# Second layer's queries projected with channels on the partitions, logits on half-height weights, and a scan's splits cut into pieces

## The chip, the cores and the metric

The kernel runs on one core of a Trainium2 chip. The metric is the device time of one execution in microseconds, and the median of several runs is compared. The core's engines have queues of their own: PE (matmuls, with PEld for loading the stationary operand, the "weights"), DVE and POOL (elementwise work), ACT (elementwise functions and copies) and SP, which issues most DMAs. SBUF is the memory in which tiles lie on 128 partitions; PSUM, eight banks of 512 fp32 columns, is where PE writes.

## The reference

A decoder of two layers on 1024 tokens of 1024 channels: a gated delta-rule layer with 8 heads, then attention over a window of 128 keys with 32 query heads of 64 channels, 4 key heads, a bias by distance and a sink. The queries are normed per head.

```python
# first layer, per head, in chunks: the scan
def step(S, inp):
    qk_i, qd_i, kd_i, u_i, w_i, gl_i = inp
    v_new = u_i - jnp.einsum("bhck,bhkv->bhcv", w_i, S)
    o = jnp.einsum("bhck,bhkv->bhcv", qd_i, S) + jnp.einsum("bhcs,bhsv->bhcv", qk_i, v_new)
    S = S * gl_i[..., None, None] + jnp.einsum("bhck,bhcv->bhkv", kd_i, v_new)
    return S, o
# second layer
q, z = jnp.split(h @ w_in, 2, axis=-1)
q = rms_norm(q.reshape(B, T, B_Q_HEADS, B_HD), q_gain) * (B_HD ** -0.5)
logits = jnp.einsum("bnqkgd,bnskd->bnkgqs", q, k_band) + bias
logits = jnp.where(mask, logits, -jnp.inf)
m = jnp.maximum(jnp.max(logits, axis=-1, keepdims=True), sink)
p = jnp.exp(logits - m)
probs = p / (jnp.sum(p, axis=-1, keepdims=True) + jnp.exp(sink - m))
o = jnp.einsum("bnkgqs,bnskd->bnqkgd", probs, v_band).reshape(B, T, B_W) * jax.nn.silu(z)
return o @ w_out
```

## The kernel before

Large products are made of three matmuls: each operand x is split into a high part hi = x rounded to the matmul's type fp32r and a low part lo = x - hi, and hi hi + hi lo + lo hi is summed in PSUM. Splits take two instructions, a rounding copy (ACT or POOL) and a subtraction (DVE). The normed input lies with channels on the partitions in `hT` (tiles hh and hl, two halves of 512 tokens).

PE's order is written out by hand. `interleave` runs a front generator and a back generator: each `yield` of the front gives a number of units, and the back then emits matmuls worth as many. `later(n, f)` emits f after n more ticks, a tick being one k step of a projection. The other engines' orders are made by a scheduler, from the order of the program, priorities and its own estimate of when operands are ready.

First layer, eight heads (`head_delta`, front; the projections of the next head are the back). After the inverse of each chunk's triangle is merged, `split` (L641) splits the decayed keys `kt` into kth (tile w0) and ktl (tile lt), and the decay-masked q k products `dm` into dmh (w1) and dml, each over all 8 chunks of 128 at once: 128x1024 on POOL (L645), then on DVE (L646). The queries are split likewise, earlier. Then the scan runs over the 8 chunks n: `r`, the new values vh and vl (ACT L804, DVE L805, whose tile is printed as lh), the state's update kth vh + ktl vh + kth vl (L813, L814, L816), and `inside` (L652 to L654), which needs dmh and dml of its chunk one chunk later.

Second layer, eight groups hg of four query heads. `b_order` is the back's order of projections: q of a group (`b_q`) and z, the gate, in two column blocks (`b_z`). `b_q` makes queries with **tokens on the partitions** (`gemm_tc`): the input is the stationary operand, 128x128, and the two query weights move, 256 columns, L971 to L973, 24 matmuls for 128 tokens. They are copied from PSUM (L1095), squared (L1097), summed by head (L1098), and scaled in place by the inverse root (L1103). A weight of a "four" kind has four k steps by 256 columns; `col` has eight by 128.

`b_attend` (front) goes through 64 blocks (X, n), X the group and n the block of 128 tokens. `q_up` splits a block's queries into hi and lo side by side (POOL L1137, DVE L1139), `q_turn` transposes them on PE, four 128x128 transposes (L1146) and a copy (L1149), so that one head's hi and lo lie stacked on 128 partitions. `logits` multiplies them by the high keys (L1167) and the low keys (L1168): eight matmuls, 256 columns (128 when n = 0), into two banks, two heads each. `key_stack` holds each group's keys twice, on partitions 0 to 63 and on 64 to 127. DVE then masks (L1169) and adds the bias, with the minimum over keys against the sink as output m (L1173); logits are kept negated. ACT takes exp with its sum (L1178), POOL multiplies by the inverse sum (L1182), `turn` transposes (L1188), `values` multiplies by v (L1209, 64 columns of the array each, two at a time). The front emits turn(i), q_turn(i+3), q_up(i+4), logits(i+2), values(i-1), with 4.8 units of back in all.

PSUM in the second layer: two banks mm for projections, three tp for transposes, two lg for logits, one pv.

Of the kernel before, what the change touches and what calls it, by code (L numbers as in the profile page):

```python
# [7 lines left out]
F32 = mybir.dt.float32  # L8
# [10 lines left out]
P = 128  # L19
# [45 lines left out]
class Kernel:  # L65
# [122 lines left out]
    def consts(self, ctx):  # L188
# [10 lines left out]
        self.identr = cp.tile([P, P], F32R, name="identr")  # L199
        nc.vector.tensor_copy(self.identr, self.ident)  # L200
# [455 lines left out]
    def head_delta(self, h, H):  # L656
# [23 lines left out]
        qh, ql = self.split(kq[:, :, 1, :], dl, "qh", dl, "ql")  # L680
        nc.gpsimd.tensor_tensor(out=kt, in0=kt, in1=self.kdec[:, :, h:h + 1].broadcast_to([P, NB, P]), op=ALU.mult)
# [87 lines left out]
        kth, ktl = self.split(kt, sm, "w0", dl, "lt")  # L769
        dmh, dml = self.split(dm, sm, "w1", dl, "dml")  # L770
# [18 lines left out]
        for n in range(NB):  # L789
# [21 lines left out]
            if n < NB - 1:  # L811
# [13 lines left out]
                nc.vector.tensor_tensor(out=Sl, in0=S, in1=self.f32(Sh), op=ALU.subtract)  # L825
                yield WAIT["state"]
# [197 lines left out]
    class Group:  # L1024


        def __init__(self, hg):
            self.hg, self.q, self.ot, self.zs, self.left = hg, [], [], [], 5

    def layer_b(self, last):  # L1030
# [7 lines left out]
        for _ in steps:  # L1038
            for _ in range(4):
                next(first)  # L1040
        for _ in first:
            pass
        self.flush()
# [5 lines left out]
        raws = lambda j: bp.tile([P, 2, 512], F32, name="qr", bufs=3)  # L1049
# [11 lines left out]
    def b_order():  # L1061

        z = [("z", hg, j) for hg in range(8) for j in range(2)]
        order = [("q", 0, 0), ("q", 1, 0), z.pop(0)]
# [15 lines left out]
    def b_q(self, X):  # L1080

        nc, bp, sb = self.nc, self.bp, self.sb
        ws = [self.take(), self.take()]
        for half in range(2):
            qr = bp.tile([P, 4, 256], F32, name="qr", bufs=3)
            ss = sb.tile([P, 4, 4], F32, name="ssqb")
            for c in range(4):
                n = half * 4 + c
                if c % 2 == 0:
                    ps = self.mm.tile([P, 2, 256], F32, name="mm")  # L1090
                yield from self.gemm_tc(ps[:, c % 2, :], ws, n)
                if c % 2 == 0:
                    continue
                two = qr[:, c - 1:c + 1, :]
                nc.vector.tensor_copy(two, ps)  # L1095
                sq = sb.tile([P, 8, 64], F32, name="sq", bufs=1)
                nc.scalar.activation(out=sq, in_=two.rearrange("p n (h d) -> p (n h) d", h=4), func=AF.Square)  # L1097
                nc.vector.tensor_reduce(out=ss[:, c - 1:c + 1, :].rearrange("p n h -> p (n h)"), in_=sq, op=ALU.add,  # L1098
                                        axis=AX.X)
            nc.vector.tensor_scalar(out=ss, in0=ss, scalar1=1.0 / 64, scalar2=EPS, op0=ALU.mult, op1=ALU.add)  # L1100
            rq = self.rsqrt(sb, ss, [P, 4, 4], "rqb")
            qv = qr.rearrange("p n (h d) -> p n h d", h=4)
            nc.vector.tensor_tensor(out=qv, in0=qv, in1=rq.unsqueeze(3).broadcast_to([P, 4, 4, 64]), op=ALU.mult)  # L1103
            X.q.append(qv)
# [21 lines left out]
    def b_attend(self, groups):  # L1126
# [3 lines left out]
        qh, qT, Ls, pTs = {}, {}, {}, {}  # L1130

        def q_up(i):
            X, n = blocks[i]
            qv = X.q[n // 4]
            c = n % 4
            t = qh[i] = bp.tile([P, 4, 2, 64], F32R, name="qh")
            nc.gpsimd.tensor_scalar(out=t[:, :, 0, :], in0=qv[:, c, :, :], scalar1=1.0, scalar2=1.0,  # L1137
                                    op0=ALU.mult, op1=ALU.mult)
            nc.vector.tensor_tensor(out=t[:, :, 1, :], in0=qv[:, c, :, :], in1=self.f32(t[:, :, 0, :]),  # L1139
                                    op=ALU.subtract)  # L1140

        def q_turn(i):
            t = qh.pop(i)
            ps = aps.tile([P, 4, P], F32R, name="tp", bufs=3)
            for e in range(4):
                nc.tensor.transpose(out=ps[:, e, :], in_=t[:, e, :, :].rearrange("p a d -> p (a d)"),  # L1146
                                    identity=self.identr)
            qT[i] = bp.tile([P, 4, P], F32R, name="qT")
            nc.scalar.copy(out=qT[i], in_=self.f32(ps))  # L1149

        def logits(i):
# [4 lines left out]
            q = qT.pop(i)  # L1156
            k0 = 0 if n else P
            ksl = slice((n - 1) * P + k0, (n + 1) * P)
            L = Ls[i] = bp.tile([P, 4, P + 1], F32, name="lsb", bufs=3)
            nc.gpsimd.tensor_copy(L[:, :, P:P + 1], sk.unsqueeze(2))  # L1160
# [235 lines left out]
```

## Time and profile before

| | us |
|---|---|
| median of 3 runs | 1869.24 (1867.32 to 1869.59) |
| profiled execution | 1867.8 |
| its span, first to last instruction | 1866.1 |
| PE busy | 1810.6 (97%) |
| PEld busy | 1486.6 (80%) |
| DVE busy | 1219.4 (65%) |
| ACT busy | 834.8 (45%) |
| POOL busy | 527.9 (28%) |

The span has the first layer's heads until about 890 us, its output projection and the shared keys and values until about 1140, the second layer until about 1690, and the last output projection. Busy time of PE is the union of overlapping matmuls: one matmul is listed at 0.28 or 0.39 us while the next starts 0.12 or 0.23 us after it. What a matmul costs is read from start to start. A list of waits names the engine and line that ended each wait of an engine that had nothing else running. The granted clock is a share of 2.4 GHz, and the other level is 1.2.

### The profile page before, as it was taken

The numbers are of one execution on the slowest core, as the hardware profiler recorded it, in microseconds if no ns is written. First come the engines' busy times: TensorE is split into PE (matmuls) and PEld (weight loads), VectorE is DVE, ScalarE is ACT, GpSimd is POOL, SyncE is SP. The second block draws the span as 40 slices with busy tenths as digits, with TensorE's granted clock in tenths as the row PEclk, the third lists the DMA queues.
The fourth block names the chain that finished last, engine by engine and source line by source line (L and its number), as shares of the span: only waits on it lengthen the run. The fifth ranks groups of instructions, "written<-read, shape, count | busy, mean of one in ns | idle before, by whom it ended". The sixth has DMA issues, their size and how long they took to land.

```text
span 1866.1 us, 30785 instructions
## 1 busy us (share of the span) xinstructions
PE 1810.6 (97%) x11650; PEld 1486.6 (80%) x11650; DVE 1219.4 (65%) x2823; ACT 834.8 (45%) x1904; POOL 527.9 (28%) x645
## 2 busy tenths in 40 slices
PE   6999999999999998999999999999999999999999
PEld 6677778787878776778788899888888888877887
DVE  6777776868586778775535365876776776743432
ACT  6446352635445364423112042557667666671100
POOL 0222222323222223221221232434434433321211
PEclk9999999999999999999999999999999999999999
DMA  4611111112011111122655331011112112215552
GB/s 151 132 51 35 57 46 46 47 35 69 24 58 34 58 34 46 46 86 82 240 169 180 114 102 46 30 46 46 57 35 63 55 32 63 68 63 209 181 172 100
DMA packets 134873, 149.54 MB, mean 80 GB/s; under 512 B 7242, under 2 KB 91716, under 8 KB 134724
## 3 DMA queue, kind: packets, MB, share of 16 engines
q1 hardware_dynamic: 124384, 130.40, 22.3%
q10 hardware_dynamic: 10340, 17.16, 3.0%
q8 instruction: 92, 1.51, 0.3%
q14 instruction: 57, 0.47, 0.1%
HBM read 116.05 MB, written 31.49 MB: 79 GB/s over the span
## 4 chain that ended last, share of the span: by engine, by line
PE 76%; DVE 10%; issue 4%; POOL 3%; ACT 1%; DMA 0%; POOLq 0%; ACTq 0%; DVEq 0%
PE mm L182 9%; PE mm L180 9%; PE mm L184 9%; PE acc L920 6%; PE acc L921 6%; PE acc L919 6%; PE mm L971 4%; PE mm L972 4%; PE mm L973 4%; PE pv L1209 3%; DVE acc L494 3%; PE lg L1168 2%; PE lg L1167 2%; PE tp L1188 1%; DVE wlo L157 1%
## 5 line engine op out<-in xcount | busy, mean ns | idle before, releaser
L180 PE MATMUL mm<-hh,whi 128*128 128x512 f32 (+1 forms) x1040 | 427.1, 411 | 2.6 <-ACT hh L246 2.5
L182 PE MATMUL mm<-hl,whi 128*128 128x512 f32 (+1 forms) x1040 | 417.8, 402 | 1.5 <-DVE hl L247 1.5
L184 PE MATMUL mm<-hh,wlo 128*128 128x512 f32 (+1 forms) x1040 | 414.7, 399 | 0.0
L157 DVE TENSOR_TENSOR wlo<-wraw,whi 128x512 fp32r<-128x512 f32 x292 | 209.4, 742 | 221.3 <-POOL whi L150 193.1
L150 POOL TENSOR_SCALAR whi<-wraw 128x1024 fp32r<-128x1024 f32 x110 | 119.8, 1090 | 482.7 <-PE acc L921 242.8
L180 PEld LDWEIGHTS mm<-hh,whi 128*128 128x128 f32 x1040 | 197.3, 190 | 37.7 <-issue 4.6
L184 PEld LDWEIGHTS mm<-hh,wlo 128*128 128x128 f32 x1040 | 197.4, 190 | 35.9 <-issue 4.2
L182 PEld LDWEIGHTS mm<-hl,whi 128*128 128x128 f32 x1040 | 197.6, 190 | 34.2 <-issue 4.2
L971 PE MATMUL mm<-whi,hh 128*128 128x256 f32 x608 | 180.0, 296 | 0.0
L494 DVE SCALAR_TENSOR_TENSOR acc<-u,cw,acc 128x512 f32<-128x512 f32 x192 | 161.7, 844 | 23.5 <-POOL acc L491 21.0
L972 PE MATMUL mm<-wlo,hh 128*128 128x256 f32 x608 | 171.8, 283 | 0.0
L973 PE MATMUL mm<-whi,hl 128*128 128x256 f32 x608 | 171.7, 282 | 0.0
L1178 ACT ACTIVATE lsb<-lsb,m 128x129 f32<-128x129 f32 x256 | 101.0, 397 | 71.3 <-DVE m L1173 42.8
L971 PEld LDWEIGHTS mm<-whi,hh 128*128 128x128 f32 x608 | 115.6, 190 | 10.9 <-issue 10.4
L972 PEld LDWEIGHTS mm<-wlo,hh 128*128 128x128 f32 x608 | 115.8, 190 | 0.2
L973 PEld LDWEIGHTS mm<-whi,hl 128*128 128x128 f32 x608 | 115.6, 190 | 0.0
L153 POOL TENSOR_TENSOR wraw<-wraw,gcolb 128x512 f32<-128x512 f32 x72 | 84.0, 1187 | 111.2 <-DMA wraw<-in_b_w_in 62.6
L1182 POOL TENSOR_TENSOR lsb<-lsb,den 128x512 f32<-128x512 f32 x64 | 69.3, 1082 | 154.1 <-DVE den L1180 134.4
L491 POOL TENSOR_SCALAR acc<-u,cw 128x512 f32<-128x512 f32 x64 | 56.3, 880 | 182.1 <-ACT u L487 168.4
L919 PE MATMUL acc<-whi,hh 128*128 128x512 f32 x256 | 99.7, 389 | 0.0
L921 PE MATMUL acc<-whi,hl 128*128 128x512 f32 x256 | 99.6, 389 | 0.0
L920 PE MATMUL acc<-wlo,hh 128*128 128x512 f32 x256 | 99.6, 389 | 0.0
(352 smaller groups left out, 3872.3 us busy)
## 6 DMA issues: line engine op xcount, KB each, us to landing
wraw<-in_a_w_in SPq DMA_DIRECT2D x48, 512.0 KB, 4.0
wraw<-in_a_w_out SPq DMA_DIRECT2D x32, 512.0 KB, 3.9
wraw<-in_b_w_in SPq DMA_DIRECT2D x32, 512.0 KB, 4.1
wraw<-in_b_w_out SPq DMA_DIRECT2D x32, 512.0 KB, 4.0
og<-zs SPq DMA_DIRECT2D x32, 256.0 KB, 2.0
ogT<-zs SPq DMA_DIRECT2D x24, 256.0 KB, 2.1
btab<-lt SPq DMA_DIRECT2D x1, 4096.0 KB, 24.2
dm<-gd SPq DMA_DIRECT2D x8, 512.0 KB, 3.7
```

The lines of the kernel that those rows point to most:

```text
L150: nc.gpsimd.tensor_scalar(out=hi, in0=raw, scalar1=1.0, scalar2=1.0, op0=ALU.mult, op1=ALU.mult)
L157: nc.vector.tensor_tensor(out=lo[:, ks], in0=raw[:, ks], in1=self.f32(hi[:, ks]), op=ALU.subtract)
L180: nc.tensor.matmul(ps, hi[:, k, :], hh[:, k, :], start=(k == 0), stop=False)
L182: nc.tensor.matmul(ps, hi[:, k, :], hl[:, k, :], start=False, stop=False)
L184: nc.tensor.matmul(ps, lo[:, k, :], hh[:, k, :], start=False, stop=(k == KT - 1))
L494: nc.vector.scalar_tensor_tensor(out=acc, in0=u[:, t:t + 512], scalar=cw[:, t, blk:blk + 1], in1=acc, op0=ALU.mult, op1=ALU.add)
L919: nc.tensor.matmul(ps[c], oh[:, k, ts], hi[:, kk, :], start=(k4 + k == 0), stop=False)
L920: nc.tensor.matmul(ps[c], oh[:, k, ts], lo[:, kk, :], start=False, stop=False)
L921: nc.tensor.matmul(ps[c], ol[:, k, ts], hi[:, kk, :], start=False, stop=(k4 + k == 6))
L971: nc.tensor.matmul(ps, hh[:, k, ts], hi[:, k % 4, :], start=(k == 0), stop=False)
L972: nc.tensor.matmul(ps, hh[:, k, ts], lo[:, k % 4, :], start=False, stop=False)
L973: nc.tensor.matmul(ps, hl[:, k, ts], hi[:, k % 4, :], start=False, stop=(k == KT - 1))
```

## The change

- **Projection.** `b_q` now makes queries with channels on the partitions, as z is made (`gemm_ct`: the weight is stationary, 512 tokens move): per group two weights (pr) by two halves by 24 matmuls of 512 columns. The weights are loaded as `col`. The split comes straight from PSUM: ACT copies to hi (tile qr), DVE subtracts to lo (tile ql). The query transposes, their splits and the rounded identity are gone.
- **Norm.** ACT squares the PSUM tile, DVE transposes it in 32x32 blocks and sums; `b_sums`, some ticks later, adds over partition groups with a small fp32 matmul against a matrix of ones, 64 columns, and makes the inverse root rq and ss = -2 ss' rq (ss' holds half the negated mean square), which is the root. Queries are not scaled any more.
- **Logits.** `rows` multiplies the bias by the root on POOL, into the tile that becomes the logits. `logits` now has twelve matmuls: for each pr, the pairs (qh kh), (ql kh), (qh kl), and in each pair one head on partitions 0 to 63 and one on 64 to 127, so on half-height weights, each head of a pair writing a bank of its own. The DVE step adds the scaled bias to the product, multiplies the sum by rq (scale) and takes the minimum as before.
- **Order.** The front's pieces are turn, logits, rows, values, again with 4.8 units. The first z moves from between q 1 and q 2 to behind q 2, and all others of its kind by one; there is no flush ahead of the attention. Tiles qr and ql have four buffers. The GpSimd DMA scratch is made smaller.
- **First layer.** `split` returns a function for a slice. Queries are split in halves, alternating with the decay of the keys. The keys and dm are split in slices of 2, 2 and 4 chunks: the first key slice ahead of the scan, the others between the scan's first four chunks.

```diff
@@ split
         hi, lo = (p.tile([P, NB, P], F32R, name=t, bufs=1) for p, t in ((ph, hi), (pl, lo)))
-        nc.gpsimd.tensor_scalar(out=hi, in0=x, scalar1=1.0, scalar2=1.0, op0=ALU.mult, op1=ALU.mult)
-        nc.vector.tensor_tensor(out=lo, in0=x, in1=self.f32(hi), op=ALU.subtract)
-        return hi, lo
+        def part(hs):
+            nc.gpsimd.tensor_scalar(out=hi[:, hs], in0=x[:, hs], scalar1=1.0, scalar2=1.0, op0=ALU.mult, op1=ALU.mult)
+            nc.vector.tensor_tensor(out=lo[:, hs], in0=x[:, hs], in1=self.f32(hi[:, hs]), op=ALU.subtract)
+        return hi, lo, part
@@ head_delta
-        kth, ktl = self.split(kt, sm, "w0", dl, "lt")
-        dmh, dml = self.split(dm, sm, "w1", dl, "dml")
+        kth, ktl, part_k = self.split(kt, sm, "w0", dl, "lt")
+        dmh, dml, part_d = self.split(dm, sm, "w1", dl, "dml")
+        part_k(some[0])
...
                 nc.vector.tensor_tensor(out=Sl, in0=S, in1=self.f32(Sh), op=ALU.subtract)
+                if n < 4:
+                    (part_d, part_k, part_d, part_d)[n](some[(0, 1, 1, 2)[n]])
+                if n == 2:
+                    part_k(some[2])
                 yield WAIT["state"]
@@ b_q
+            part = sb.tile([P, 2, 16], F32, name="part")
+            for pr in range(2):
+                ps = self.mm.tile([P, 512], F32, name="mm")
+                yield from self.gemm_ct(ps, ws[pr], half)
+                if pr == 0:
+                    hi = bp.tile([P, 2, 512], F32R, name="qr", bufs=4)
+                    lo = bp.tile([P, 2, 512], F32R, name="ql", bufs=4)
+                nc.scalar.copy(out=hi[:, pr, :], in_=ps)
+                sq = sb.tile([P, 8, 64], F32, name="sq", bufs=1).rearrange("p n d -> p (n d)")
+                nc.scalar.activation(out=sq, in_=ps, func=AF.Square)
+                nc.vector.tensor_tensor(out=lo[:, pr, :], in0=ps, in1=self.f32(hi[:, pr, :]), op=ALU.subtract)
+                sqT = sb.tile([P, 512], F32, name="sqT", bufs=1)
+                nc.vector.transpose(out=sqT, in_=sq)
+                nc.vector.tensor_reduce(out=part[:, pr, :], in_=sqT.rearrange("p (b c) -> p b c", c=32), op=ALU.add,
                                         axis=AX.X)
+            X.q.append((hi, lo))
+            self.later(5, lambda part=part: self.b_sums(X, part))
+
+    def b_sums(self, X, part):
...
+        ps = self.aps.tile([P, 512], F32, name="tp", bufs=3)[:, 0:64]
+        nc.tensor.matmul(ps, self.same, two.rearrange("p r a b -> p (r a b)"), start=True, stop=True)
...
+        rq = self.rsqrt(sb, ss, [P, 4, 4], "rqb")
+        nc.vector.scalar_tensor_tensor(out=ss, in0=ss, scalar=-2.0, in1=rq, op0=ALU.mult, op1=ALU.mult)
+        X.norm.append((rq, ss))
@@ b_attend
+        def rows(i):
             X, n = blocks[i]
...
+            rms = X.norm[n // 4][1][:, :, n % 4:n % 4 + 1]
+            nc.gpsimd.tensor_tensor(out=L[:, :, 0:P], in0=X.bias, in1=rms.broadcast_to([P, 4, P]), op=ALU.mult)
...
+            pss = [aps.tile([P, 2, 256], F32, name="lg") for _ in range(2)]
             for pr in range(2):
-                ps = aps.tile([P, 2, 256], F32, name="lg")
-                for j in range(2):
-                    e = 2 * pr + j
-                    nc.tensor.matmul(ps[:, j, k0:256], q[:, e, :], kh[:, ksl], start=True, stop=False)
-                    nc.tensor.matmul(ps[:, j, k0:256], q[:, e, :], kl[:, ksl], start=False, stop=True)
+                for w, k in ((qh, kh), (ql, kh), (qh, kl)):
+                    for a in range(2):
+                        rs = slice(64 * a, 64 * a + 64)
+                        nc.tensor.matmul(pss[a][:, pr, k0:256], w[rs, pr, :], k[rs, ksl], start=(w is qh and k is kh),
+                                         stop=(k is kl))
...
-        fill = (1.2, 1.2, 0.6, 0.6, 1.2)
+        fill = (2.4, 0.6, 0.6, 1.2)
```

PE's queue before, in the middle of the second layer, at a block's query transposes (mm is a projection's bank, tp a transpose bank, lg a logits bank; numbers are tiles):

```order
L973 MATMUL mm_13259<-whi_12958,hl0_86 128x256
L1146 MATMUL tp_13357<-identr_75,qh_13273 128x128 x4
L971 MATMUL mm_13389<-whi_12770,hh1_87 128x256
L972 MATMUL mm_13389<-wlo_12771,hh1_87 128x256
L973 MATMUL mm_13389<-whi_12770,hl1_88 128x256
```

and, nine projection matmuls later,

```order
L973 MATMUL mm_13389<-whi_12770,hl1_88 128x256
L1167 MATMUL lg_13405<-kh_12625,qT_13271 128x256
L1168 MATMUL lg_13405<-kl_12626,qT_13271 128x256
L1167 MATMUL lg_13405<-kh_12625,qT_13271 128x256
L1168 MATMUL lg_13405<-kl_12626,qT_13271 128x256
L1167 MATMUL lg_13413<-kh_12625,qT_13271 128x256
L1168 MATMUL lg_13413<-kl_12626,qT_13271 128x256
```

PE's queue now, at a block's logits (qr is the high part of the queries, ql the low part):

```order
L182 MATMUL mm_13145<-hl0_83,whi_12766 128x512
L1184 MATMUL lg_13152<-kh_12491,qr_12085 128x256
L1184 MATMUL lg_13153<-kh_12491,qr_12085 128x256
L1184 MATMUL lg_13152<-kh_12491,ql_12086 128x256
L1184 MATMUL lg_13153<-kh_12491,ql_12086 128x256
L1184 MATMUL lg_13152<-kl_12492,qr_12085 128x256
L1184 MATMUL lg_13153<-kl_12492,qr_12085 128x256
```

These six stand there twice, for pr 0 and 1. The transposes have left the queue, the logits fill two banks in turns, and the projections' matmuls are half as many and twice as wide.

DVE's queue before, head 5, from the key split to the state of the scan's first chunk (lt is ktl, w the POOL side of a split, acc the next head's convolution, lh is vl):

```order
L591 TENSOR_TENSOR kt<-kt,rky 128x1024
L646 TENSOR_TENSOR lt<-kt,w_7031 128x1024
L494 SCALAR_TENSOR_TENSOR acc<-u,cw,acc 128x512
L646 TENSOR_TENSOR dml<-dm,w_7035 128x1024
L805 SCALAR_TENSOR_TENSOR lh<-sc,beta,Z 128x256
```

and now:

```order
L589 TENSOR_TENSOR kt<-kt,rky 128x1024
L646 TENSOR_TENSOR lt<-kt,w_7087 128x256 x2
L646 TENSOR_TENSOR lt<-kt,w_7087 128x512
L646 TENSOR_TENSOR dml<-dm,w_7089 128x256 x2
L492 SCALAR_TENSOR_TENSOR acc<-u,cw,acc 128x512
L646 TENSOR_TENSOR dml<-dm,w_7089 128x512
L810 SCALAR_TENSOR_TENSOR lh<-sc,beta,Z 128x256
```

The two subtractions have become six, five of them written behind the first chunk's own work in the program; on the queue all six stand ahead of lh.

## Rows read from the trace of the kernel before

**Rows 1.** Windows: busy us (instructions) by engine, granted clock, DMA share, GB/s.

```profile
60.00:890.00 830.00, 798.83 (x5532) 635.78 (x5531) 605.45 (x1202) 379.89 (x848) 214.34 (x240) 0.99 0.20 55
1140.00:1690.00 550.00, 547.96 (x3797) 463.36 (x3796) 382.46 (x1228) 355.41 (x892) 208.69 (x303) 1.00 0.17 53
1165.00:1170.00 5.00, 4.67 (x29) 4.47 (x28) 5.00 (x17) 1.85 (x9) 3.34 (x4) 0.66 0.00 1
```

**Rows 2.** PE's waits, 1140 to 1690 us: total us, times, longest us.

```profile
PE lg L1167 <- DVE rqbt L118: 0.9, 1, 0.9
PE lg L1167 <- DVE m L1173: 0.8, 1, 0.8
```

**Rows 3.** PE's waits, 60 to 890 us.

```profile
PE sc L816 <- DVE lh L805: 12.1, 15, 1.9
```

**Rows 4.** PE's timeline, a query transpose: start us, duration us, engine, line, operation, tiles.

```profile
1187.35 0.46 PE L1146 MATMUL tp<-identr,qh 128*128 128x128 f32 x4
1187.64 0.35 PE L971 MATMUL mm<-whi,hh 128*128 128x256 f32 x1
1187.83 0.28 PE L972 MATMUL mm<-wlo,hh 128*128 128x256 f32 x1
1187.95 0.28 PE L973 MATMUL mm<-whi,hl 128*128 128x256 f32 x1
```

**Rows 5.** PE's timeline, first logits matmul of a block, first matmul behind the eight.

```profile
1180.90 0.28 PE L1167 MATMUL lg<-kh,qT 128*128 128x256 f32 x1
...
1181.85 0.28 PE L971 MATMUL mm<-whi,hh 128*128 128x256 f32 x1
```

**Rows 6.** PE's timeline, the values matmuls between projection matmuls.

```profile
1190.68 0.28 PE L973 MATMUL mm<-whi,hl 128*128 128x256 f32 x1
1190.88 1.08 PE L1209 MATMUL pv<-pT,vv 128*64 128x256 f32 x8
1191.90 0.39 PE L971 MATMUL mm<-whi,hh 128*128 128x256 f32 x1
1192.12 0.28 PE L972 MATMUL mm<-wlo,hh 128*128 128x256 f32 x1
```

**Rows 7.** PE's timeline, first layer: corner matmuls in pairs, and on one corner.

```profile
236.83 1.15 PE L687 MATMUL kqp<-w 64*64 64x64 f32 x32
...
243.21 1.14 PE L761 MATMUL kqp<-w,lt 64*64 64x64 f32 x16
```

**Rows 8.** PE's timeline, logits of a group's first block, matmul behind them.

```profile
1221.40 0.22 PE L1167 MATMUL lg<-kh,qT 128*128 128x128 f32 x1
...
1222.24 0.33 PE L971 MATMUL mm<-whi,hh 128*128 128x256 f32 x1
```

**Rows 9.** PE's timeline, first layer, around a small ones-matrix matmul.

```profile
150.29 0.39 PE L184 MATMUL mm<-hh,wlo 128*128 128x512 f32 x1
150.52 0.29 PE L552 MATMUL tr<-part,cst 128*128 128x16 f32 x2
150.66 0.47 PE L180 MATMUL mm<-hh,whi 128*128 128x512 f32 x1
150.97 0.39 PE L182 MATMUL mm<-hl,whi 128*128 128x512 f32 x1
```

**Rows 10.** POOL's lines, 1140 to 1690 us: busy us, mean ns, idle before.

```profile
L1182 POOL TENSOR_TENSOR lsb<-lsb,den 128x512 f32<-128x512 f32 x64 | 69.3, 1082 | 154.1 <-DVE den L1180 134.4 <-DVE rqby L111 9.4 <-DVE rqbt L118 9.1
...
L1137 POOL TENSOR_SCALAR qh<-qr 128x256 fp32r<-128x256 f32 x64 | 28.7, 448 | 28.1 <-PE tp L1146 13.7 <-DVE qr L1103 13.1 <-PE tp L1188 1.3
```

**Rows 11.** Timeline of POOL and DVE in head 5, the scan's splits.

```profile
656.24 1.04 POOL L645 TENSOR_SCALAR w<-dm 128x1024 fp32r<-128x1024 f32 x1 [0.96 <-PE kqp L766]
656.28 2.08 DVE L646 TENSOR_TENSOR lt<-kt,w 128x1024 fp32r<-128x1024 f32 x1
...
658.94 1.21 DVE L646 TENSOR_TENSOR dml<-dm,w 128x1024 fp32r<-128x1024 f32 x1
```

**Rows 12.** Lines of the whole span: a DVE split of 256 columns.

```profile
L825 DVE TENSOR_TENSOR XT<-S,X 128x256 fp32r<-128x256 f32 x56 | 24.1, 431 | 15.3 <-ACT X L824 15.3
```

More of the change, by code (lines that the diff above doesn't have):

```diff
@@ L679, in head_delta @@
                                 channel_multiplier=-1)
-        qh, ql = self.split(kq[:, :, 1, :], dl, "qh", dl, "ql")
-        nc.gpsimd.tensor_tensor(out=kt, in0=kt, in1=self.kdec[:, :, h:h + 1].broadcast_to([P, NB, P]), op=ALU.mult)
+        some = (slice(0, 2), slice(2, 4), slice(4, 8))
+        qh, ql, part_q = self.split(kq[:, :, 1, :], dl, "qh", dl, "ql")
+        for hs in (slice(0, 4), slice(4, 8)):
+            part_q(hs)
+            nc.gpsimd.tensor_tensor(out=kt[:, hs], in0=kt[:, hs], in1=self.kdec[:, hs, h:h + 1].broadcast_to([P, 4, P]),
+                                    op=ALU.mult)
         blocks = [(n, r) for n in range(NB) for r in (0, 64)]
@@ L1038, in layer_b @@
         for _ in steps:
-            for _ in range(4):
+            for _ in range(12):
                 next(first)
@@ L1063, in b_order @@
         z = [("z", hg, j) for hg in range(8) for j in range(2)]
-        order = [("q", 0, 0), ("q", 1, 0), z.pop(0)]
+        order = [("q", 0, 0), ("q", 1, 0)]
         for hg in range(2, 8):
@@ L1084, in b_q @@
         for half in range(2):
[L1085 to L1098, printed above, removed]
-                                        axis=AX.X)
@@ new lines, in b_q @@
+            X.q.append((hi, lo))
+            self.later(5, lambda part=part: self.b_sums(X, part))
+    def b_sums(self, X, part):
+        nc, sb = self.nc, self.sb
+        two = sb.tile([P, 2, 2, 16], F32, name="two")
+        first = self.cst[:, C_TRI + 63:C_TRI + 64]
+        nc.vector.tensor_scalar(out=two[:, :, 0, :], in0=part, scalar1=first, scalar2=None, op0=ALU.mult)
+        nc.vector.tensor_tensor(out=two[:, :, 1, :], in0=part, in1=two[:, :, 0, :], op=ALU.subtract)
+        ps = self.aps.tile([P, 512], F32, name="tp", bufs=3)[:, 0:64]
+        nc.tensor.matmul(ps, self.same, two.rearrange("p r a b -> p (r a b)"), start=True, stop=True)
+        two = two.rearrange("p r a b -> p (r a) b")
+        nc.vector.tensor_tensor(out=two, in0=ps.rearrange("p (e b) -> p e b", e=4), op=ALU.mult,
+                                in1=self.group.unsqueeze(1).broadcast_to([P, 4, 16]))
+        ss = sb.tile([P, 4, 4], F32, name="ssqb")
+        nc.vector.tensor_reduce(out=ss, in_=two.rearrange("p e (n g) -> p e n g", g=4), op=ALU.add, axis=AX.X)
+        nc.vector.tensor_scalar(out=ss, in0=ss, scalar1=1.0 / 64, scalar2=EPS, op0=ALU.mult, op1=ALU.add)
+        rq = self.rsqrt(sb, ss, [P, 4, 4], "rqb")
+        nc.vector.scalar_tensor_tensor(out=ss, in0=ss, scalar=-2.0, in1=rq, op0=ALU.mult, op1=ALU.mult)
+        X.norm.append((rq, ss))
@@ L1129, in b_attend @@
         blocks = [(X, n) for X in groups for n in range(NB)]
-        qh, qT, Ls, pTs = {}, {}, {}, {}
-        def q_up(i):
+        Ls, pTs = {}, {}
+        def rows(i):
             X, n = blocks[i]
[L1134 to L1149, printed above, removed]
+            L = Ls[i] = bp.tile([P, 4, P + 1], F32, name="lsb", bufs=3)
+            nc.gpsimd.tensor_copy(L[:, :, P:P + 1], self.sink[:, 4 * X.hg:4 * X.hg + 4].unsqueeze(2))
+            rms = X.norm[n // 4][1][:, :, n % 4:n % 4 + 1]
+            nc.gpsimd.tensor_tensor(out=L[:, :, 0:P], in0=X.bias, in1=rms.broadcast_to([P, 4, P]), op=ALU.mult)
         def logits(i):
@@ L1215, in b_attend @@
         last = len(blocks) - 1
[L1216 to L1218 removed]
+        rows(0)
+        rows(1)
         yield 1.0
         logits(0)
[L1221 to L1222 removed]
+        rows(2)
         yield 1.5
         logits(1)
[L1225 to L1226 removed]
         yield 2.5
[L1228 removed]
+        fill = (2.4, 0.6, 0.6, 1.2)
         steps = iter(())
@@ L1232, in b_attend @@
             yield fill[0]
-            if i + 3 <= last:
-                q_turn(i + 3)
-            if i + 4 <= last:
-                q_up(i + 4)
-            yield fill[1]
             if i + 2 <= last:
                 logits(i + 2)
-            yield fill[2]
+            if i + 3 <= last:
+                rows(i + 3)
+            yield fill[1]
             if X.hg < 7:
@@ L1364, in weights @@
                 for k in range(2):
-                    yield four(bin_, k, hg, gain(2 + k))
+                    yield col(bin_, 2 * hg + k, self.gcolb[:, 8:16])
             else:
```

42 lines of the change are left out of this document (14 added, 28 removed).

## The prediction

> **What bounds the kernel now.** I read the windows first, then PE's waits by stage, then PE's timeline step by step. The windows split the program into the first layer's heads (60 to 890 us) and the second layer (1140 to 1690 us) [rows 1]. In the second layer PE is busy 547.96 of 550 us while DVE, ACT and POOL are busy 382, 355 and 209 us. Only three PE waits are listed there, two of which are shown, 0.9 and 0.8 us, both of logits matmuls as the attention starts [rows 2]. They are followed by a stretch whose granted clock is 0.66 [rows 1], so part of it ran at 1.2 GHz instead of 2.4. Apart from that PE hardly waits: **the second layer is as long as the steps on PE's queue**, and an instruction removed from another engine buys nothing there. In the first layer PE is busy 799 of 830 us; the largest single wait is L816 for the low half of the new values (`vl`, printed as lh, L805), 12.1 us in 15 waits [rows 3].
>
> Busy times of matmuls overlap, so I price PE by the distance from one start to the next.
>
> **Query transposes removed.** Each block's four L1146 transposes take from 1187.35 to 1187.64, 0.29 us. The projection matmul after them also starts its successor 0.19 us later instead of 0.12 [rows 4]. That is 0.36 us a block, 64 blocks: **-23 us**. The copies, splits and casts that go with them are off the path.
>
> **Logits by rows.** Before, eight matmuls of 256 columns take 1180.90 to 1181.85, 0.95 us, or 0.119 us each, with no extra step at either end [rows 5]. Now there are twelve, in six pairs. One of a pair uses rows 0 to 63 of the array, the other rows 64 to 127, each writing a bank of its own. The price hangs on two things that no row shows for this shape.
>
> First, whether the two of a pair run side by side. The nearest rows: L687, 32 fp32 matmuls in pairs on two 64x64 corners of the array, spans 1.15 us, and L761, 16 of them on one corner, spans 1.14 us [rows 7]. The second corner costs nothing, in its loads of weights or in its columns. But those pairs differ in their columns as well as their rows; the new ones share all 128 columns. I take side by side, the side that the rows are nearer to: six pairs, 0.71 us.
>
> Second, what entering and leaving half an array costs. The values matmuls (L1209) use half the columns. The last projection matmul before them lasts 0.20 us instead of 0.12, and after them the first lasts 0.22 instead of 0.12 [rows 6]. An exit step is hidden in their 1.02 us; I give it the price of the entry, 0.09. Together 0.28 us a block. So the new logits cost 0.99 against 0.95, +0.04 for 56 blocks. The eight first blocks of a group have 128 columns and take 1221.40 to 1222.24, 0.84 us or 0.105 each [rows 8]. They become 0.63 + 0.28 = 0.91. Together **+2.8 us**. With no switching cost at all it would be 56 x (0.71 - 0.95) + 8 x (0.63 - 0.84) = -15; with no overlap 56 x (1.43 + 0.28 - 0.95) + 8 x (1.26 + 0.28 - 0.84) = +48. Those are the ends.
>
> On the switching, the Trainium skill, "TensorEngine Tiling (Array Packing)", section Key Properties, says that a change of tiling mode drains TensorE. The steps around L1209 agree; by the rule the logits come out at +2.8, without it at -15.
>
> **Projection turned.** A group's queries were 192 matmuls of 256 columns at 0.119, 22.8 us; now 96 of 512 columns. Row L184 of 512 columns hands over after 0.23 us [rows 9], 22.1 us. Eight groups: -5.6 by rounded steps; I take **-5 us**.
>
> **Norm sums added.** Sixteen small fp32 matmuls (`b_sums`). The nearest row is L552, the same ones matrix with 16 columns: 150.52 to 150.66, and the next step 0.31 instead of 0.23 [rows 9], 0.22 us. With 64 columns between that and 0.30; at 0.24 that is **+3.8 us**.
>
> **Work behind PE in the second layer.** POOL gains one multiplication of 128x512 a block, nearest row L1182 at 1082 ns, and loses L1137 at 448 ns [rows 10]: +41 us on 209 of 550 busy. DVE loses the PSUM copy, the scaling and the query split, and gains a subtract, a transpose, a reduce and the small sums, about as much as it loses. ACT loses 64 copies. All stay below PE, so I cost this at nothing; the cover is the distance of two blocks between a block's logits and its transposes, less than two periods of 550 / 64 = 8.6 us. Both logits banks now go to one block at once, so a block's DVE work on them must end before the next block's first pair, not its second half. All of DVE's work is 382 / 64 = 6.0 us a block, of which this is a part. At the start of the attention the second logits will wait for the first block's DVE work, as before [rows 2]. I put 0 there, with 3 us either way, since a wait of that size decides whether the half-clock stretch comes.
>
> **Pieces in the first layer.** The aim is plain: `vl` is behind the splits on DVE's queue. But the second order excerpt shows all the pieces still ahead of it in a typical head: the scheduler moves what is ready. So nothing is taken off the queue; the pieces only change its cost. At head 5, POOL's split (1.04 us at 656.24) holds up DVE's, which takes 2.08 us beside it and 1.21 alone [rows 11]: the two do not run side by side, so finer pieces are not simply a finer pipeline. A piece of 256 takes 448 ns on POOL [rows 10] and 431 on DVE [rows 12]. Against a quarter of 1.04 and 1.21 that is 0.19 and 0.13 us of fixed cost a piece. Two more pieces in each of two splits: up to 1.27 us a head later, +10 us over eight heads. The other end: DVE waits only for a half after POOL's last piece, 1.21 - (0.61 + 0.13) = 0.48 us earlier a head, -4 us. The middle is +3; I take **+1.5 us**, since the fixed part of a piece on one of the two engines can pass while the other has its turn.
>
> **Sum.** -23 + 2.8 - 5 + 3.8 + 0 + 1.5 = -19.9 us. The profiled execution took 1867.8 us, so 1847.9; the median of the runs is 1869.24, 1.4 us more. Forecast **1849 us**.
>
> **Rivals.**
> - *The pairs run one after the other.* For it: the two share the columns, and the 128-column logits show that 0.105 us is the floor for a matmul with a new 128-column weight, whatever it multiplies [rows 8]. Against it: the corner pairs [rows 7]. Price: +48 instead of +2.8, so 1849 + 45 = **1894 us, slower**. It decides from the point where the second of a pair adds 0.06 us, half its own time: 20 us over 64 blocks of six pairs is 0.05. Beside it, the Trainium skill, "TensorE: Matmul & The Clock Gate", section LDWEIGHTS (loading the stationary operand), says that a load goes by its columns and not its rows, so half-height weights load no faster. The floor of rows 8 fits that; whether two such loads overlap no run here shows.
> - *Switching costs nothing for rows:* -15 instead of +2.8, **1831 us**. Against it the steps around L1209 [rows 6].
> - *The pieces cost their full fixed part:* +10 instead of +1.5, **1857 us**. The waits of L816 [rows 3] would become more than 15.
> - *The second layer waits for POOL or DVE:* if half of the 0.63 us that POOL gains a block lands on PE, +20 us, **1869 us**, no change; all of it, 1889. Against it the shares of rows 1.
> - *The pieces do what they are for:* at most all 12.1 us of the waits for `vl` go [rows 3], instead of +1.5: 1835 us. The order speaks against it; it lies in the range.
>
> **How the numbers follow.** Forecast with its own spread (1835 to 1857) 0.58, of which the last rival has 0.05; no switching cost 0.10; pieces dear 0.12; pairs in turn 0.12; second layer waiting 0.08, half of it slower and half the same. A measurement of this kernel tells about 0.2%, 3.7 us, from no change. Faster by more: 0.58 + 0.10 + 0.12 = 0.80, less 0.01 for both dear at once, 0.79; slower 0.12 + 0.04 = 0.16; same 0.05. The range leaves out the pairs in turn and most of the waiting, 0.18, and below it 0.02: 1830 to 1866 us.
>
> **What would show it.** In the timeline after, a pair's two starts a few ns apart and pairs about 0.12 us from each other mean side by side. Steps of 0.11 to 0.12 for each matmul mean in turn. The steps next to the logits should read about 0.2 and 0.22 where now there are 0.12; no L1146 rows; projection steps of 0.23. In the list of waits, L816 near 12 us, no wait of a logits or transpose matmul beyond the first blocks, and the second layer's PE still busy for 99% of it, at the full clock. I am wrong if the attention's length falls by less than 15 us while the pairs overlap, since then something else than PE has become the bound there, or if the first layer's end moves by more than 10 us.

## The result, and the profile after

The changed kernel takes **1895.82 us** (median of 4, 1893.85 to 1897.71) against 1868.85 (4 runs beside it): ratio **1.0147**, 95% interval 1.0135 to 1.0159. It is slower by 27 us, where 20 us less were forecast. The profiled execution took 1896.8 us, its span 1895.0.

The loss lies in the second layer. From its first key matmul (L971, now L981) to the last values matmul it took 606.1 us before (1081.5 to 1687.6) and takes 636.2 (1080.1 to 1716.3). The scan ends 1.4 us earlier, and the last projection takes 174 us in both.

The windows of the profile after, to set beside [rows 1]:

```profile
core 0: us, PE busy (x) PEld busy (x) DVE busy (x) ACT busy (x) POOL busy (x), PEclk, DMA share, GB/s
60.00:890.00 830.00, 799.29 (x5534) 637.15 (x5534) 606.48 (x1244) 381.06 (x851) 231.15 (x287) 0.99 0.19 56
1140.00:1720.00 580.00, 548.79 (x3092) 393.97 (x3091) 390.35 (x1263) 337.20 (x861) 239.89 (x303) 0.97 0.17 51
```

PE's work in the second layer is 548.8 us, as much as before, but it now stretches over 580 us, and the granted clock is 0.97 where it was 1.00. PE's waits there, against [rows 2]:

```profile
PE tp L1122 <- DVE two L1120: 29.1, 13, 5.6
PE lg L1184 <- DVE m L1192: 2.1, 2, 1.8
```

**L1122 is the matmul of the norm sums.** Thirteen of its sixteen calls make PE stand still for 29.1 us in all, up to 5.6 at a time. PE's queue at one of them:

```profile
1236.40 0.40 PE L182 MATMUL mm<-hl,whi 128*128 128x512 f32 x1
1236.63 0.40 PE L184 MATMUL mm<-hh,wlo 128*128 128x512 f32 x1
1241.16 0.69 PE L1122 MATMUL tp<-two,cst 128*128 128x64 f32 x2 [4.13 <-DVE two L1120]
1241.61 0.77 PE L180 MATMUL mm<-hh,whi 128*128 128x512 f32 x1
```

and DVE's in the same stretch:

```profile
1235.67 0.69 DVE L1215 TENSOR_TENSOR pT<-tp,cst 128x512 f32<-128x512 f32 x1 [0.69 <-PE tp L1207]
1237.35 0.22 DVE L1127 TENSOR_REDUCE ssqb<-two 128x16 f32<-128x64 f32 x1 [0.98 <-POOL lsb L1165]
1237.48 0.68 DVE L1105 TENSOR_TENSOR ql<-mm,qr 128x512 fp32r<-128x512 f32 x1
1238.08 0.16 DVE L1128 TENSOR_SCALAR ssqb<-ssqb 128x16 f32<-128x16 f32 x1
1238.16 0.70 DVE L1108 STREAM_TRANSPOSE sqT<-sq 128x512 f32<-128x512 f32 x1
1238.89 0.69 DVE L1109 TENSOR_REDUCE part<-sqT 128x16 f32<-128x512 f32 x1
1239.61 0.48 DVE L1119 TENSOR_SCALAR two<-part,cst 128x32 f32<-128x32 f32 x1
1240.13 0.98 DVE L1120 TENSOR_TENSOR two<-part,two 128x32 f32<-128x32 f32 x1
```

ACT copied the projection's bank from 1234.47 on. PE has no more than five ticks of other work until L1122 and reaches it at 1236.86. The operand `two` needs the transpose, the reduce and two small steps on DVE, which itself first waits for a transpose of the attention and then for POOL, in L1127, the step that writes the norm tile of the half before: `two` is there at 1241.11. With nothing in the way (the first call, at 1146.0) the chain still takes 3.65 us from ACT's copy; in the attention it takes 4.1 to 8.9.

The wait has a second price. The first projection matmul behind it lasts 0.77 us, where it lasts 0.47 without the wait (e1 below, at 1150.96), and the next one 0.63 instead of 0.39. The window around them:

```profile
1239.80:1246.60 6.80, 5.44 (x21) 4.10 (x22) 2.39 (x6) 0.00 (x0) 1.26 (x2) 0.51 0.01 2
```

The granted clock is 0.51 here, 1.2 GHz. It was 1.00 up to 1239.9, when PE had stood still for about 3 of the 4.1 us. The second layer now has seven such stretches, 34 us in all, where before it had one of 3.4. At half the clock that is 17.0 us lost now and 1.7 before. Five of the seven, 13.6 us lost, begin in or just behind the five longest waits of L1122, 3.4 to 5.6 us each. Of the other two, one comes at the start of the attention, as before, and one at 1089.7, ahead of the attention. PE stands still for 3.6 of the 34 us, so 1.8 of the 17.0 us are in the waits as well.

What was forecast to come did come: no query transposes, projection steps of 0.23 us, and the pairs side by side:

```profile
1404.88 0.40 PE L184 MATMUL mm<-hh,wlo 128*128 128x512 f32 x1
1405.21 0.39 PE L1184 MATMUL lg<-kh,qr 64*128 64x256 f32 x2
1405.43 0.28 PE L1184 MATMUL lg<-kh,ql 64*128 64x256 f32 x2
1405.55 0.28 PE L1184 MATMUL lg<-kl,qr 64*128 64x256 f32 x2
1405.67 0.28 PE L1184 MATMUL lg<-kh,qr 64*128 64x256 f32 x2
1405.79 0.28 PE L1184 MATMUL lg<-kh,ql 64*128 64x256 f32 x2
1405.91 0.28 PE L1184 MATMUL lg<-kl,qr 64*128 64x256 f32 x2
1406.12 0.50 PE L180 MATMUL mm<-hh,whi 128*128 128x512 f32 x1
1406.45 0.39 PE L182 MATMUL mm<-hl,whi 128*128 128x512 f32 x1
1406.69 0.40 PE L184 MATMUL mm<-hh,wlo 128*128 128x512 f32 x1
```

A pair (x2) starts as one, and pairs follow at 0.12 us, as six of [rows 5] would. But the block costs more: from 1404.88 to 1406.69 are 1.81 us, less three projection steps of 0.23 leaves **1.11 us**, where 0.99 was forecast. The price of the half-height form shows in four steps, not three: 0.33 ahead, 0.22 in the first pair, 0.21 behind the last, 0.33 in the next projection matmul, 0.39 us beyond the plain steps.

### The profile page after: what moved, and what is told of

The parts are those of the page before. It is cut to its first block, busy times and chain, and to the rows that moved or that the text cites. A ratio compares the mean times of both kernels' runs of the same rounds, so it can differ in the third digit from the quotient of the medians.

```text
span 1895.0 us, 29395 instructions
## 1 busy us (share of the span) xinstructions
PE 1810.5 (96%) x10914; PEld 1416.1 (75%) x10914; DVE 1227.4 (65%) x2894; ACT 816.0 (43%) x1872; POOL 576.7 (30%) x693
## 5 line engine op out<-in xcount | busy, mean ns | idle before, releaser
L180 PE MATMUL mm<-hh,whi 128*128 128x512 f32 (+1 forms) x1296 | 537.0, 414 | 2.5 <-ACT hh L244 2.5
L182 PE MATMUL mm<-hl,whi 128*128 128x512 f32 (+1 forms) x1296 | 523.9, 404 | 1.5 <-DVE hl L245 1.5
L184 PE MATMUL mm<-hh,wlo 128*128 128x512 f32 (+1 forms) x1296 | 521.6, 402 | 0.0
L180 PEld LDWEIGHTS mm<-hh,whi 128*128 128x128 f32 x1296 | 247.9, 191 | 55.0 <-issue 9.7
L184 PEld LDWEIGHTS mm<-hh,wlo 128*128 128x128 f32 x1296 | 246.9, 191 | 52.5 <-issue 8.1
L182 PEld LDWEIGHTS mm<-hl,whi 128*128 128x128 f32 x1296 | 247.5, 191 | 49.1 <-issue 7.3
L1192 DVE CUSTOM_DVE_ANT_0 lsb<-lg,lsb,sink 128x128 f32<-128x128 f32 x256 | 90.5, 404 | 0.2
L929 PE MATMUL acc<-whi,oh 128*128 128x512 f32 x192 | 76.0, 396 | 0.0
L931 PE MATMUL acc<-whi,ol 128*128 128x512 f32 x192 | 75.9, 395 | 0.0
L930 PE MATMUL acc<-wlo,oh 128*128 128x512 f32 x192 | 75.6, 394 | 0.0
```

The costliest lines, as they stand in the source:

```text
L180: nc.tensor.matmul(ps, hi[:, k, :], hh[:, k, :], start=(k == 0), stop=False)
L182: nc.tensor.matmul(ps, hi[:, k, :], hl[:, k, :], start=False, stop=False)
L184: nc.tensor.matmul(ps, lo[:, k, :], hh[:, k, :], start=False, stop=(k == KT - 1))
L929: nc.tensor.matmul(ps[c], oh[:, k, ts], hi[:, kk, :], start=(k4 + k == 0), stop=False)
L930: nc.tensor.matmul(ps[c], oh[:, k, ts], lo[:, kk, :], start=False, stop=False)
L931: nc.tensor.matmul(ps[c], ol[:, k, ts], hi[:, kk, :], start=False, stop=(k4 + k == 6))
```

## The experiments

"e1" below is the first kernel, which the later ones build on. All ratios are against the kernel before.

**1. The place of the sums (e1), the norm tiles, both.**

```diff
-            self.later(5, lambda part=part: self.b_sums(X, part))
+            self.later(14, lambda part=part: self.b_sums(X, part))
```

> The norm sums are put 14 ticks behind their half's projection instead of 5; nothing else differs from the changed kernel. Theory (sums too early in PE's queue): the small matmul L1122 stands only 5 ticks of 0.69 us, 3.5 us, behind the last projection matmul of its half, while its operand needs ACT's copy and square (0.56 + 0.59) and DVE's transpose, reduce and two small steps (0.70 + 0.69 + 0.24 + 0.19) after it, 3.0 us with no other work in the way; DVE has other work, so PE waited 29.1 us in 13 waits, and half-clock stretches followed. 14 ticks are 9.7 us: the waits of L1122 fall below 3 us, the half-clock stretches in the second layer go with them, and the time is about 1852 us (1846 to 1860). Rival (norm tiles held): DVE's reduce L1127 waits for POOL's rows L1165, 24.7 us in 11, since the norm tile ssqb has two buffers and the rows of two halves back must have read theirs; DVE's queue then holds up the next half's chain. By it a later matmul takes away only a part: PE still waits 10 to 20 us, about 1875 to 1885 us. Third (clock alone, not the waits, or something else in the attention): no change from 1896.

Measured: **1856.65 us** (1854.22 to 1859.30), ratio 0.9938 [0.9923, 0.9953]. One number takes away 39 us. L1122 now stands 9 to 20 us behind the start of ACT's copy, against chains of 3.7 to 10.6, and no wait of it is left in the list:

```profile
PE lg L1184 <- DVE m L1192: 4.7, 3, 3.4
PE tp L1207 <- POOL lsb L1201: 0.8, 1, 0.8
PE lg L1184 <- DVE two L1120: 0.8, 1, 0.8
```

The time lost to the clock in the second layer falls to 3.4 us. And without its wait the small matmul costs what was forecast, 0.24:

```profile
1150.58 0.40 PE L184 MATMUL mm<-hh,wlo 128*128 128x512 f32 x1
1150.82 0.33 PE L1122 MATMUL tp<-two,cst 128*128 128x64 f32 x2
1150.96 0.47 PE L180 MATMUL mm<-hh,whi 128*128 128x512 f32 x1
1151.27 0.39 PE L182 MATMUL mm<-hl,whi 128*128 128x512 f32 x1
```

1150.58 to 1151.27 is 0.69, less two projection steps: 0.23 us.

```diff
-        ss = sb.tile([P, 4, 4], F32, name="ssqb")
+        ss = sb.tile([P, 4, 4], F32, name="ssqb", bufs=4)
-        rq = self.rsqrt(sb, ss, [P, 4, 4], "rqb")
+        rq = self.rsqrt(sb, ss, [P, 4, 4], "rqb", bufs=4)
```

> The two norm tiles (ss and the inverse root) get four buffers instead of two; the sums stay 5 ticks behind the projection. Theory (norm tiles held by POOL's rows): DVE's wait of L1127 on POOL's L1165, 24.7 us in 11, goes to zero, the chain behind it on DVE runs on time, the waits of L1122 fall from 29 us to below 8, and the time is about 1855 us (1850 to 1866). Rival (sums too early in PE's queue): DVE's wait goes all the same, but the chain of 3.0 us still stands behind DVE's other work and meets a slot 3.5 us behind the projection, so PE still waits 15 us or more in L1122: 1875 to 1893 us.

Measured: 1884.69 us (1883.20 to 1886.06), 1.0088 [1.0072, 1.0103]. DVE's wait in L1127 (24.7 us in 11 in the changed kernel) is gone, and PE's wait shrinks, but stays:

```profile
PE tp L1122 <- DVE two L1120: 18.9, 13, 3.1
```

So the norm tiles were a real part, 11 us, but most of the wait is there without them. With both edits:

> Both edits together: 14 ticks and four buffers of the norm tiles. If the waits of L1122 and the half-clock stretches behind them are all that stands between the forecast and the result, this is the forecast, 1849 us (1843 to 1855), whichever of the two edits does it. If the time stays above 1860, a further cost that I have not named is in the second layer.

Measured: 1858.27 us (1858.01 to 1860.85), 0.9949 [0.9935, 0.9964], the same as e1. Once PE comes late enough, it doesn't matter that DVE waits for POOL in L1127 (13.9 us in 6 in e1, none in e3_both). Both stay above the forecast by 8 to 9 us, for which the ledger below accounts.

> Norm sums 9 ticks behind their projection (5 in the changed kernel, 14 in e1_delay14); nothing else. Theory (a slot that comes too early in PE's queue, against a chain on ACT and DVE of a given length): each of the waits of L1122 gets shorter by the 4 ticks, 2.8 us, or vanishes. The gaps ahead of L1122 in the changed kernel, less 0.33 us, were 5.6, 4.5, 4.2, 4.0, 3.5, 3.0 and ten under 1.7 us; what is left is about 8 us in 6, and the half-clock stretches behind the short ones go: 1862 to 1872 us. If the sums' place does not matter above some point, or the waits come from something that follows the matmul wherever it is, as the norm tiles would, the waits stay above 15 us and the time above 1878.

Measured: 1859.43 us (1858.22 to 1860.75), 0.9953 [0.9939, 0.9968]. Better than I expected, with 2.0 us of waits left instead of 8:

```profile
PE tp L1122 <- DVE two L1120: 1.3, 2, 1.0
PE tp L1122 <- DVE rqbt L117: 0.7, 1, 0.7
```

I had counted four ticks as 2.8 us; the attention's own matmuls lie between ticks, so in the trace L1122 now mostly stands 7 to 10 us behind the start of ACT's copy, against chains of 3.7 to 8.8. The dose orders as the theory says: 1896, 1859, 1857 at 5, 9 and 14 ticks, though the last two agree within their spread.

**2. The price of the half-height logits.** All on e1.

```diff
-            for pr in range(2):
-                for w, k in ((qh, kh), (ql, kh), (qh, kl)):
-                    for a in range(2):
+            for a in range(2):
+                for pr in range(2):
+                    for w, k in ((qh, kh), (ql, kh), (qh, kl)):
```

> The kernel of e1_delay14 with the same twelve logits matmuls in another order: the six of the heads on partitions 0 to 63 first, then the six on 64 to 127, so that only one pair of neighbours lies on different rows. It prices the overlap of pairs alone. If pairs side by side are worth a step of 0.117 us each, five of the six are lost: 5 x 0.117 x 56 + 5 x 0.113 x 8 = 37 us over e1_delay14, about 1894 us. If the order of the twelve does not matter, 1857 us.

Measured: 1875.20 us (1872.11 to 1877.88), 1.0042 [1.0028, 1.0056]: 18.5 us over e1, half of what I expected. The timeline tells why:

```profile
1250.71 0.38 PE L1184 MATMUL lg<-kh,qr 64*128 64x256 f32 x1
1250.93 0.28 PE L1184 MATMUL lg<-kh,ql 64*128 64x256 f32 x1
1251.05 0.28 PE L1184 MATMUL lg<-kl,qr 64*128 64x256 f32 x1
1251.06 0.39 PE L1184 MATMUL lg<-kh,qr 64*128 64x256 f32 x2
1251.28 0.29 PE L1184 MATMUL lg<-kh,ql 64*128 64x256 f32 x2
1251.40 0.29 PE L1184 MATMUL lg<-kl,qr 64*128 64x256 f32 x2
1251.51 0.28 PE L1184 MATMUL lg<-kh,qr 64*128 64x256 f32 x1
```

In the queue stand six matmuls of one half, then six of the other. In the trace three run alone, three beside three, three alone: nine steps, not eleven. Three steps more than e1 are 22 us over 64 blocks; PE's waits are 2.5 us shorter than in e1 (3.8 for 6.3), and the clock takes 1.7 us less. The order of issue took away only half of the overlap, so I took away all of it by the operands:

```diff
-                        rs = slice(64 * a, 64 * a + 64)
+                        rs = slice(0, 64)
```

> The kernel of e1_delay14 with all twelve logits matmuls on partitions 0 to 63, in the same order; the second head of each pair gets the first one's logits, so the output is other than the reference's. It takes the overlap away altogether: twelve steps instead of six. In e6_in_turn the trace showed nine steps instead of six (the matmuls on rows 64 to 127 started after three of the other half, though six stood ahead of them), and 18.5 us more than e1_delay14. Six more steps are 6 x 0.117 x 56 + 6 x 0.113 x 8 = 45 us: 1901 us. If a step's length came from something else than the rows, 1857 to 1875.

Measured: **1900.40 us** (1897.61 to 1901.93), 1.0170 [1.0154, 1.0186], 43.8 over e1. On one half of the rows the pairs come 0.24 us apart instead of 0.12:

```profile
1288.67 0.40 PE L1184 MATMUL lg<-kh,ql 64*128 64x256 f32 x2
1288.91 0.40 PE L1184 MATMUL lg<-kl,qr 64*128 64x256 f32 x2
```

Running side by side is worth 44 us here.

```diff
+                nc.tensor.matmul(pss[0][:, pr, k0:256], qh[:, pr, :], kh[:, ksl], start=True, stop=False)
+                nc.tensor.matmul(pss[0][:, pr, k0:256], ql[:, pr, :], kh[:, ksl], start=False, stop=True)
+                nc.tensor.matmul(pss[1][:, pr, k0:256], qh[:, pr, :], kl[:, ksl], start=True, stop=True)
```

> The kernel of e1_delay14 with six logits matmuls over all 128 rows in place of the six pairs: the two heads' products are summed, so the logits are not those of one head and the output is other than the reference's; banks, columns and what reads them stay. It prices entering and leaving the half-height form. The trace of e1_delay14 has 1.11 us a block for six pairs (0.09 before, 0.10 in the first pair, 0.09 behind the last, 0.11 in the next projection matmul over six steps of 0.119): without these the block is 0.71, so 56 x 0.40 + 8 x 0.35 = 25 us less than e1_delay14, about 1831 us. By the prediction's 0.28 a block it is 18 us less, 1839. If entering and leaving costs nothing that the end sees, 1857.

Measured: 1836.19 us (1831.72 to 1839.58), 0.9827 [0.9809, 0.9846], 20.5 below e1, between the two expectations. By its steps the block is 0.40 us shorter (1.40 for logits and three projection steps, 1.81 in the excerpt further up), 25 us in all:

```profile
1257.15 0.40 PE L182 MATMUL mm<-hl,whi 128*128 128x512 f32 x1
1257.38 0.28 PE L1181 MATMUL lg<-kh,qr 128*128 128x256 f32 x1
...
1258.55 0.39 PE L182 MATMUL mm<-hl,whi 128*128 128x512 f32 x1
```

Of that 3.8 us come back as waits of PE (10.1 where e1 has 6.3), and 1.7 by the clock. So 0.39 us a block is the price of the form, and four fifths of it reach the end.

```diff
-        fill = (2.4, 0.6, 0.6, 1.2)
+        fill = (2.4, 0.0, 0.0, 2.4)
```

> The kernel of e1_delay14 with the projection work of a block parted otherwise: units 2.4, 0, 0, 2.4 in place of 2.4, 0.6, 0.6, 1.2, so that the half-height logits of one block and the half-width values of another stand side by side on PE, with no full-size projection matmul between them. In e1_delay14 each of the two pays its own way out and in: behind the logits 0.09 in the last step and 0.11 in the next projection matmul, ahead of the values 0.09, then 0.05 in the first pair. If PE goes from one form to the other in a single step of 0.1 to 0.2 us, 0.15 to 0.25 us a block are saved, 10 to 16 us: 1841 to 1847. If it must empty itself twice, 1857. Against it: DVE and ACT get a block's logits and transposes closer together, and a new wait of PE on them could take all of it: above 1857.

Measured: **1853.00 us** (1850.93 to 1853.90), 0.9916 [0.9901, 0.9931], the lowest median that still computes the reference, 3.6 below e1, though the two intervals overlap. PE does go from one form to the other in one short step:

```profile
1268.96 0.28 PE L1184 MATMUL lg<-kl,qr 64*128 64x256 f32 x2
1269.17 1.08 PE L1228 MATMUL pv<-pT,vv 128*64 128x256 f32 x8
1270.19 0.50 PE L180 MATMUL mm<-hh,whi 128*128 128x512 f32 x1
```

From the last pair 0.21 to the values, and no step of 0.33 between: beyond plain projection steps, logits and values together take 2.11 us instead of 1.11 + 1.21, 0.2 less, 13 us over 64 blocks. Most of it was given back, 1.7 us by the clock (5.1 against 3.4) and 5.3 as waits, 11.6 us where e1 has 6.3:

```profile
PE lg L1184 <- DVE m L1192: 6.1, 6, 3.4
PE tp L1207 <- POOL lsb L1201: 3.9, 6, 1.9
PE lg L1184 <- DVE two L1120: 1.6, 2, 0.8
```

I then moved the transposes, with units 1.6, 0, 0, 3.2:

> As e9_adjacent, with the units of projection work parted 1.6, 0, 0, 3.2: the transposes of a block come 0.8 us later against its logits, which stay beside the values. e9_adjacent saved 0.20 us on PE in each block, 13 us by the steps of its trace, but came out only 3.6 us faster than e1_delay14, with 3.9 us of waits of the transposes for POOL's division (0.8 before) and 7.7 us of waits of the logits (5.5 before). If the waits of the transposes are a matter of distance, those 3.9 us go and the time is 1847 to 1851 us. If the two sorts of waits only change places, 1853.

Measured: 1856.28 us (1852.88 to 1861.64), 0.9939 [0.9924, 0.9953]: no gain. The waits for POOL fell from 3.9 to 0.3 us, those of the logits rose from 7.7 to 11.9. They changed places. That also says what is next behind PE: a block's way through DVE, ACT and POOL no longer fits everywhere in the distance that PE leaves it.

**3. The start of the attention, and the first layer.**

```diff
         rows(2)
-        yield 1.5
+        yield 5.5
         logits(1)
```

> The kernel of e1_delay14 with 5.5 units of projection work in place of 1.5 between the first two blocks' logits. In e1_delay14 the second block's logits wait 3.4 and 1.0 us for DVE's step on the first block, as both logits banks hold that block, and a half-clock stretch of some 7 us follows, 3.4 us of PE's time. If that wait is the cause of the stretch, both go: 8 us less, about 1849 us. If the 4 us of projection work that were moved ahead are missed at the end of the attention, 4 us of it come back: 1853. If the stretch comes anyway, 1853 too, but with the granted clock showing it.

Measured: 1864.28 us (1861.09 to 1868.22), 0.9977 [0.9968, 0.9987], **7.6 slower** than e1. The waits up to 1250 shrank from 5.5 to 3.5 us, but between 1250 and 1550 there are 7.2 us, where e1 has 0.8, and at the end the last two blocks' values stand alone:

```profile
1677.31 1.08 PE L1228 MATMUL pv<-pT,vv 128*64 128x256 f32 x8
1678.86 1.08 PE L1228 MATMUL pv<-pT,vv 128*64 128x256 f32 x8 [0.47 <-ACT ot L1230]
```

Projection work used up early is missing later. The half-clock stretch came all the same, 3.4 us instead of 6.8. All in all PE's waits are 12.2 us against 6.3 and the clock takes 1.7 us less, which is 4.2 of the 7.6; the rest is open.

The pieces of the first layer, put into the kernel before:

> The kernel before with only the first layer's splits cut in pieces, everything else as it was. My step: +1.5 us against the kernel before, from -4 to +10. The first layer of the changed kernel ended 1.4 us earlier than before, with 10.8 us in 14 waits of the last state matmul for vl instead of 12.1 in 15; if that is the pieces' doing, this run is 1 to 2 us faster than the kernel before, about 1867.5 us. The rival that the pieces take vl's waits off: 1857 us, with those waits near zero. The rival that each piece pays its full fixed part: 1878 us.

Measured: 1866.34 us (1862.32 to 1869.66), 0.9989 [0.9979, 0.9999]; and taken out of e1:

> The kernel of e1_delay14 with the first layer's splits whole again, as in the kernel before. e4_pieces alone was 1.7 us faster than the kernel before, interval 0.9979 to 0.9999. If that is the pieces' doing, this run is 1 to 3 us slower than e1_delay14, 1858 to 1860 us. If the pieces cost the 1.5 us of the prediction, it is faster, 1855. The waits of the last state matmul for vl tell how: 12 us in 15 whole, about 11 in 14 in pieces.

Measured: 1859.21 us (1856.22 to 1861.09), 0.9949 [0.9935, 0.9963], 2.6 over e1. Both point to a gain of about 2 us, but neither is far from noise: e4_pieces' interval ends at 0.9999, and that of e11_whole_splits overlaps e1's. The waits for `vl` that the pieces were meant to remove hardly change. They are 12.1 us in 15 with whole splits ([rows 3], and again in e11_whole_splits), and in e4_pieces

```profile
PE sc L823 <- DVE lh L812: 10.9, 14, 2.2
```

## Why the prediction was wrong

- **What bounds the kernel** was right: the second layer is as long as PE's queue. What I did not draw from it is that whatever is put *into* that queue with an operand of another engine becomes part of the bound.
- **Norm sums** is the step that failed. I priced sixteen matmuls, +3.8 us, from a row of the first layer [rows 9], and they cost 0.23 us each, as said. I gave no wait to them. Yet the diff says `later(5, ...)`: five ticks of 0.69 us, while the operand's chain was ACT's copy and square and four DVE steps. The trace before could price it: its first layer has the same transpose and reduce, at 0.70 and 0.68 us (L546, L548), and a square on ACT takes 0.63 (L1097). That comparison, distance against chain, was left out. It cost 29.1 us directly, and moving the sums alone took 39 us off (e1).
- **"I cost this at nothing; the cover is the distance of two blocks"** covered the wrong chain. It held for logits to transposes, which wait nowhere in the list of the changed kernel (its logits wait 2.1 us for m). The sums had a cover of their own, 3.5 us, and I never named it.
- **Half clock.** I allowed 3 us for a stretch at the start. The waits made five more: 17.0 us lost in all instead of 1.7.
- **Logits by rows:** mechanism right, size wrong, +9.9 instead of +2.8 (56 x 0.16 + 8 x 0.12). Side by side was right, and the price I gave for the other case, 45 us, is what e10_one_half measured (43.8). Switching is 0.39 instead of 0.28 us: I took an entry and two exits and left out the first pair's own step. The values had shown it: within the 1.02 us of [rows 6], which I called hidden, the trace has steps of 0.27, 0.22, 0.22 and 0.31. By the Trainium skill, "TensorEngine Tiling (Array Packing)", section Key Properties, a change of mode drains TensorE. The trace agrees in so far as each change costs a step, 0.39 us for the way there and back.
- **Projection** and **query transposes** came as forecast: no rows of the latter, steps of 0.23 for the former.
- **Pieces:** -1.7 and -2.6 instead of +1.5, inside the -4 to +10 given, with the sign on the other side. As forecast nothing was taken off the queue: in the trace after, seven of eight heads run all pieces of the keys and of dm ahead of the scan's first vl.
- **The sign of being wrong** that I had set came: the second layer's length did not fall by 15 us but grew by 30, while the pairs overlap. What took PE's place there was the chain on ACT and DVE.
- **Rivals.** The result lies at the 1894 of *pairs in turn*, but by chance: in the changed kernel no pair ran in turn. What happened is nearest to *the second layer waits for POOL or DVE*, at another place, with some 43 us (waits and clock) where I gave 20 or 40, and with a chance of 0.08.

The ledger closes: -23 (transposes) + 9.9 (logits) - 5 (projection) + 3.7 (sums) + 29.1 (their waits) + 15.3 (clock) - 1.7 (pieces) = +28.3, or +26.5 without the 1.8 us that stand in both the waits and the clock; measured +27.0. The -23 and -5 are the forecast's own terms, not measured alone. e1, by the same terms without the sums' waits: -23 + 9.9 - 5 + 3.7 + 1.7 (clock) + 4.3 (6.3 us of other waits, 2.0 before) - 1.7 = -10.1; measured 1856.65 - 1868.04 = -11.4.

## What to carry to other kernels

When a matmul enters the queue of the engine that bounds the kernel, price its wait before its work: put the distance from its operand's source, in that queue's own time, beside the operand's chain on the other engines with their queues, and place it behind the longest such chain. The longest stalls here, 3.4 to 5.6 us, were paid twice, once in waiting and once in the clock behind them. And when an array form is changed for a short run, count all four steps around it. Setting two such runs side by side saved 0.2 us of PE's time a block here, though the waits took much of it back.

## What was not expected of the hardware

- **Matmuls on the two halves of the rows overlap without being neighbours in the queue.** In e6_in_turn those on rows 64 to 127 began after three of the other half, with three that stood ahead of them in the queue still to start. The Trainium skill, "TensorE: Matmul & The Clock Gate", part "Packing small matmuls — row/col tiling", section The mechanism, says that matmuls start and end strictly in program order. This trace shows otherwise for the starts, and the time, 18.5 us instead of 37, bears the trace out.
- **The small DVE steps of the norm are slow beside POOL.** L1120 (128x32) has a median of 0.19 us and a longest of 1.04; in the excerpt above it takes 0.98. Both slow calls, at 1218.92 and 1240.13, begin 0.05 and 0.11 us behind the start of a POOL step of 1.04 us on 128x512, and end 0.05 us behind its end. L117, 128x16, a step behind the sums' matmul, goes from 0.14 to 1.05. L1120 lies in the sums' chain; L117 lies on the same queue.
- **From half-height to half-width in 0.21 us.** Going straight from one partial form to the other costs one short step, where going through the full array costs about 0.2 us more.
